# A decoder layer in one core: the sweep in pieces of 384 or 272 tokens, and the cross branch's output projection moved behind it

## The chip, the cores and the metric

The kernel runs on one core of a Trainium2 chip. The metric is the device time of one execution in microseconds; lower is better. The engines are TensorE (PE; its weight loads are listed as PEld), VectorE (DVE), ScalarE (ACT), GpSimd (POOL) and the queue engine SP. Each runs its own instructions in their order. DMAs are issued from SP, ACT and POOL, and a DMA that has to wait holds up what stands behind it on the engine that issues it.

## What is computed

One layer of a decoder with three parallel branches, for 2048 prompt tokens and 32 sample tokens (T = 2080 in all), in float32. Cut to what matters:

```
h = rmsnorm(x, g_pre) @ w_in          # 1024 -> 9472 columns: q k v za | ub zb | qc zc | gt
oa = three dilated window attentions per head, combined          # 12 heads x 64
ob = silu(layernorm(causal_conv(glu(ub))))                       # 768 channels
oc = softmax(qc @ mem_k.T) @ mem_v                               # 4 heads x 128, 256 memory rows
gates = sigmoid(gt)                                              # 3 x 1024
mix = (gates[0] * ((oa * silu(za)) @ w_pa)
     + gates[1] * ((ob * silu(zb)) @ w_pb)
     + gates[2] * ((oc * silu(zc)) @ w_pc))
y = x + rmsnorm(mix @ w_out, g_post)
```

The outputs are y, the new rows of keys and values, the convolution's state and the memory keys and values. Branch A is the attention, B the convolution, C the cross-attention; the numbers 0, 1 and 2 of the code stand for them. The sigmoids come out of tanh: a gate is held as tanh(x / 2), and one is added where it is used; factors of a half cancel in the last normalization.

## The kernel before, in words

Everything lies with channels on the 128 partitions and tokens along the free axis. Each float32 matrix product is done as three fast ones: both sides are split into a high and a low half, and `gemm` (lines 156 to 164) adds hi x hi, hi x lo and lo x hi in one PSUM tile, three matmuls for each 128 rows of the contraction. The weights of a block of 128 output columns are loaded and split by `load_w` (lines 141 to 154; the high half on POOL or ACT, the low one on POOL).

- **Phase A1** normalizes x into tiles x0 to x2 (three thirds of the tokens: 768, 768, 544) and runs the blocks of w_in for q, k, v, the convolution's input and qc, with pieces of 384, 256 or 288 tokens (`CHUNKS`, tile `g`). The second and third third of x are also kept in DRAM (`d_x`).
- **The sweep** (`sweep`, lines 1064 to 1081) runs the other 40 blocks of w_in: za (6), zb (6), zc (4), gt (24), over the thirds one after the other, each block again for each third. It takes `SCHUNKS`, seven pieces of 256 tokens and one of 288; each is 24 matmuls in tile `gg`. `chunk` evicts a piece: gt by one tanh on ACT (line 237), z blocks by a tanh on ACT (239) and a multiplication on VectorE (240), into tile `st` and from there to DRAM (242, on ACT's queue): `d_za`, `d_zb`, `d_zc`, and `d_g`, which has 8 tiles for each branch. `st` and the PSUM pool of `gg` have two buffers each. At a change of third the tiles x0h0 to x0h7 and x0l0 to x0l7 are loaded again by POOL's queue (1072).
- **Beside the sweep** run the convolution's normalization and the memory attention, the attention of the sample tokens, and then the prompt's attention, 12 heads in six pairs. At the end of a pair its three patterns are weighted: an exponential (422), coefficients to DRAM (430), from there into `cb` (437), multiplications, and a store to `d_act` (443).
- **Phase C** (`phase_c`) goes over four parts of 512, 512, 512 and 544 tokens. In each part it takes the branches in the order C, B, A: it loads the branch's output (`araw`, 1125) and its gate path (`z`, 1127), multiplies (1128), splits the product into `ac` tiles (1186, 1187), and for each of 8 blocks of columns loads a weight block (`craw`, 146; `chi`, `clo` 150, 151), multiplies in tile `pg`, and adds gate times product to `mix` (1139 for C, 1142 and 1144 for B and A). Behind the last branch come the product with w_out (tile `y`) and the normalization.

What sets the order: the instructions are written in program order (memory, sample attention, attention, sweep, phase C), and a scheduler that works from a simulated timeline sets them in the order of each engine. What was written earlier goes first when it is ready, and the sweep fills the rest. `d_` tensors lie in DRAM.

## Time and profile before

| | us |
|---|---|
| median of 3 runs | 3169.32 (3164.48 to 3171.83) |
| the profiled execution | 3156.1 |
| its span, first to last instruction | 3154.0 |
| TensorE busy | 2992.8 |
| VectorE / POOL / ACT busy | 2037.6 / 1368.9 / 1123.6 |
| sweep matmuls (tile gg), 7680, time with one running | 1092.6, between 850 and 2557 |
| phase C's first matmul | 2558.8 |

A row of a group gives the line, the engine, the operation, what it writes and reads, the shape and the count; behind the bar the time in which one ran, the mean of one in ns, and the engine's idle time just before such instructions with what ended it. Matmuls overlap in the pipeline, so the mean of one is longer than the distance to the next. Rows of stretches give start and end, length, then for each engine the busy time and the count, the clock that was granted to TensorE, the share of the 16 DMA engines and GB/s. Rows of the timeline give start, length, engine, line, operation, operands, count and in brackets the idle time before with what ended it; a q behind the engine (ACTq) is its sequencer that issues a DMA. Rows of waits give sum, times and longest.

### The profile page before, as it was taken

How to read it: one execution, taken by the hardware profiler on the slowest of the kernel's cores; microseconds unless marked ns; L12 is line 12 of the kernel's file. 1: busy time of each engine (PE TensorE's matmuls, PEld its weight loads, DVE VectorE, ACT ScalarE, POOL GpSimd, SP SyncE). 2: the span in 40 equal slices, each digit the busy share in tenths (PEclk: the TensorE clock that was granted, in tenths of full speed). 3: DMA queues.
4: the chain of work that ended last, by engine and by line, in shares of the span. 5: the costliest groups of instructions: out<-in, count | busy, mean ns of one | idle time of the engine just before them, and what ended most of it. 6: DMA issues, size and time to landing. Idle time of an engine off the chain costs nothing. (4 is left out here: it accounts for less than half of the span.)

```text
span 3154.0 us, 55551 instructions
## 1 busy us (share of the span) xinstructions
PE 2992.8 (95%) x20705; PEld 2837.2 (90%) x20705; DVE 2037.6 (65%) x3854; ACT 1123.6 (36%) x2835; POOL 1368.9 (43%) x1048
## 2 busy tenths in 40 slices
PE   7999999999977999999999999999999989999998
PEld 6899999999977899998999999999898967787897
DVE  5297797797677825565546667565757557555663
ACT  5110010010132423244447575665565532222221
POOL 0121322232455537444366666667776443233240
PEclk9999999999998999999999999999999999999999
DMA  6332222221255444468454556575655486657561
GB/s 224 111 100 83 80 60 61 63 63 64 90 162 166 127 140 144 147 213 251 144 142 118 151 139 159 123 196 144 166 140 149 117 283 210 226 172 220 158 206 53
DMA packets 532219, 454.67 MB, mean 144 GB/s; under 512 B 118191, under 2 KB 458581, under 8 KB 531137
## 3 DMA queue, kind: packets, MB, share of 16 engines
q1 hardware_dynamic: 357502, 335.36, 36.3%
q10 hardware_dynamic: 169840, 105.02, 11.6%
q0 software_dynamic: 4608, 10.75, 1.1%
q8 instruction: 164, 2.69, 0.4%
q14 instruction: 105, 0.86, 0.1%
HBM read 332.96 MB, written 118.04 MB: 143 GB/s over the span
## 5 line engine op out<-in xcount | busy, mean ns | idle before, releaser
L162 PE MATMUL gg<-x0h,whi 128*128 128x256 f32 (+1 forms) x2560 | 747.9, 292 | 33.9 <-DVE st L240 26.9
L164 PE MATMUL gg<-x0h,wlo 128*128 128x256 f32 (+1 forms) x2560 | 741.1, 290 | 5.7 <-POOL wlo L56 5.7
L163 PE MATMUL gg<-x0l,whi 128*128 128x256 f32 (+1 forms) x2560 | 742.3, 290 | 0.0
L55 POOL TENSOR_SCALAR whi<-wraw 128x1024 fp32r<-128x1024 f32 x162 | 221.4, 1368 | 918.0 <-PE g L163 534.7
L162 PEld LDWEIGHTS gg<-x0h,whi 128*128 128x128 f32 x2560 | 493.7, 193 | 42.2 <-DVE st L240 23.5
L164 PEld LDWEIGHTS gg<-x0h,wlo 128*128 128x128 f32 x2560 | 493.6, 193 | 8.3 <-POOL wlo L56 6.1
L163 PEld LDWEIGHTS gg<-x0l,whi 128*128 128x128 f32 x2560 | 493.9, 193 | 1.9 <-issue 0.3
L316 DVE SCALAR_TENSOR_TENSOR acc<-G,cw,acc 128x1536 f32<-128x1536 f32 (+15 forms) x354 | 461.8, 1336 | 0.0
L56 POOL TENSOR_TENSOR wlo<-wraw,whi 128x1024 fp32r<-128x1024 f32 x162 | 451.8, 2790 | 9.9 <-PE gg L164 0.5
L151 POOL TENSOR_TENSOR clo<-craw,chi 128x768 fp32r<-128x768 f32 (+1 forms) x96 | 172.6, 1799 | 352.9 <-ACT chi L150 338.1
L616 ACT ACTIVATE P<-T,stm 128x128 f32<-128x128 f32 (+1 forms) x576 | 260.7, 455 | 116.7 <-DVE stm L614 78.1
L233 ACT ACTIVATE st<-g 128x384 f32<-128x384 f32 (+1 forms) x132 | 60.3, 461 | 564.8 <-PE g L164 564.8
L614 DVE CUSTOM_DVE_ANT_0 T<-s,bias 128x128 f32<-128x128 f32 (+1 forms) x576 | 191.8, 357 | 78.3 <-PE s L606 44.6
L162 PE MATMUL pg<-ac,chi 128*128 128x512 f32 (+1 forms) x640 | 227.7, 358 | 14.9 <-ACT chi L150 7.9
L164 PE MATMUL pg<-ac,clo 128*128 128x512 f32 (+1 forms) x640 | 227.8, 358 | 6.2 <-POOL clo L151 6.2
L163 PE MATMUL pg<-ac,chi 128*128 128x512 f32 (+1 forms) x640 | 227.7, 356 | 0.7 <-DVE ac L1187 0.7
L164 PE MATMUL g<-x1h,wlo 128*128 128x384 f32 x544 | 186.2, 343 | 0.0
L163 PE MATMUL g<-x1l,whi 128*128 128x384 f32 x544 | 185.9, 342 | 0.0
L162 PE MATMUL g<-x1h,whi 128*128 128x384 f32 x544 | 183.0, 339 | 3.0 <-ACT x1h L131 3.0
L163 PE MATMUL g<-x0l,whi 128*128 128x384 f32 x544 | 184.9, 340 | 0.0
L164 PE MATMUL g<-x0h,wlo 128*128 128x384 f32 x544 | 183.7, 338 | 0.0
L162 PE MATMUL g<-x0h,whi 128*128 128x384 f32 x544 | 182.5, 337 | 0.0
(329 smaller groups left out, 7453.4 us busy)
## 6 DMA issues: line engine op xcount, KB each, us to landing
wraw<-in_w_in ACTq DMA_DIRECT2D x119, 512.0 KB
d_g<-st ACTq DMA_DIRECT2D x168, 128.0 KB
cb<-d_cf SPq DMA_DIRECT2D x72, 256.0 KB
g<-d_g SPq DMA_DIRECT2D x72, 256.0 KB
wraw<-in_w_in SPq DMA_DIRECT2D x35, 512.0 KB
kvc<-in_cache_k_win SPq DMA_DIRECT2D x8, 1536.0 KB
kvc<-in_cache_v_win SPq DMA_DIRECT2D x8, 1536.0 KB
raw<-d_q SPq DMA_DIRECT2D x48, 256.0 KB
```

The source lines that it names most:

```text
L55: nc.gpsimd.tensor_scalar(hi, raw, 1.0, 1.0, op0=ALU.mult, op1=ALU.mult)
L56: nc.gpsimd.tensor_sub(lo, raw, hi.bitcast(F32))
L151: nc.gpsimd.tensor_sub(lo, raw, hi.bitcast(F32))
L162: nc.tensor.matmul(ps, hi[:, k, :], h, start=k == 0, stop=False)
L163: nc.tensor.matmul(ps, hi[:, k, :], l, start=False, stop=False)
L164: nc.tensor.matmul(ps, lo[:, k, :], h, start=False, stop=k == kb - 1)
L233: nc.scalar.activation(st[:, :n], p[:, :n], AF.Copy, scale=sc)
L316: nc.vector.scalar_tensor_tensor(a3[:, lo:hi], G[:, src:src + hi - lo, 2 - m:130 - m], w, a3[:, lo:hi], op0=ALU.mult, op1=ALU.add)
L614: nc.vector.tensor_tensor_reduce(sc[:, :w], t[:, o:o + w], bias[:, 256 - w:256], 1.0, 3.0e38, ALU.add, ALU.min, m)
L616: nc.scalar.activation(P[:, o:o + w], sc[:, :w], AF.Exp, bias=m, scale=-1.0, accum_out=self.stl[:, col:col + 1])
```

## The change

`SCHUNKS` now has four pieces of 384 tokens and two of 272, two pieces in each third. Branch C's projection is taken out of phase C. A new function `branch_c` runs it behind the sweep, in the sweep's tiles: for each third it loads the four outputs of the cross-attention into x0h4 to x0h7 and the four gate paths into x0l4 to x0l7 (POOL's queue), multiplies, and splits into x0h0 to x0h3 and x0l0 to x0l3; for each of 8 column blocks it loads and splits a weight block in the sweep's weight tiles, and for each piece it loads the gate into an `st` tile (ACT's queue), does 12 matmuls in `gg`, multiplies in the `st` tile and stores it to the new DRAM tensor `d_mix` (ACT's queue). Phase C loads `mix` from `d_mix` beside branch B's gates and adds B and A to it.

```diff
-SCHUNKS = [(256 * i, 256) for i in range(7)] + [(1792, 288)]
+SCHUNKS = [(384 * i, 384) for i in range(4)] + [(1536, 272), (1808, 272)]
...
+    def branch_c(self, xp, wp, stg, ps):
+
+        nc, I = self.nc, self.I
+        for th, (a, n) in enumerate(THIRDS):
+            acts = []
+            for k in range(4):
+                raw, z, h, l = (xp.tile([128, 768], R32, name=t)[:, :n]
+                                for t in (f"x0h{4 + k}", f"x0l{4 + k}", f"x0h{k}", f"x0l{k}"))
+                raw, z = raw.bitcast(F32), z.bitcast(F32)
+                nc.gpsimd.dma_start(raw, self.d_act[12 + k][:, a:a + n])
+                nc.gpsimd.dma_start(z, self.d_zc[k][:, a:a + n])
+                nc.vector.tensor_mul(raw, raw, z)
+                nc.scalar.activation(h, raw, AF.Copy)
+                nc.vector.tensor_sub(l, raw, h.bitcast(F32))
+                acts.append((h, l))
+            for cb in range(8):
+                raw = stg.tile([128, 8, 128], F32, name="wraw", bufs=2)[:, :4]
+                hi, lo = (wp.tile([128, 8, 128], R32, name="w" + c)[:, :4] for c in ("hi", "lo"))
+                nc.scalar.dma_start(raw, I["w_proj_c"][0, :, 128 * cb:128 * cb + 128].rearrange("(k p) n -> p k n", p=128))
+                self.split_pool(hi, lo, raw)
+                for s, m in SCHUNKS:
+                    if a <= s < a + n:
+                        g = stg.tile([128, 384], F32, name="st")
+                        nc.scalar.dma_start(g[:, :m], self.d_g[16 + cb][:, s:s + m])
+                        p = ps.tile([128, 512], F32, name="gg")
+                        self.gemm(p[:, :m], (hi, lo), [(h[:, s - a:s - a + m], l[:, s - a:s - a + m]) for h, l in acts])
+                        nc.vector.scalar_tensor_tensor(g[:, :m], g[:, :m], 1.0, p[:, :m], op0=ALU.add, op1=ALU.mult)
+                        nc.scalar.dma_start(self.d_mix[cb][:, s:s + m], g[:, :m])
+                        yield
...
+                    if br == 1:
+                        nc.sync.dma_start(mix[cb][:, :n], self.d_mix[cb][:, s:s + n])
...
-                for bi, (br, k0, kb, wn) in enumerate(((2, 12, 4, "w_proj_c"), (1, 6, 6, "w_proj_b"), (0, 0, 6, "w_proj_a"))):
+                for br, k0, kb, wn in ((1, 6, 6, "w_proj_b"), (0, 0, 6, "w_proj_a")):
...
-                            if bi == 0:
-                                nc.vector.scalar_tensor_tensor(mix[cb][:, o:o + m], g[:, :m], 1.0, p[:, :m],
-                                                               op0=ALU.add, op1=ALU.mult)
-                            else:
-                                nc.vector.scalar_tensor_tensor(g[:, :m], g[:, :m], 1.0, p[:, :m],
-                                                               op0=ALU.add, op1=ALU.mult)
-                                nc.vector.tensor_add(mix[cb][:, o:o + m], mix[cb][:, o:o + m], g[:, :m])
+                            nc.vector.scalar_tensor_tensor(g[:, :m], g[:, :m], 1.0, p[:, :m], op0=ALU.add, op1=ALU.mult)
+                            nc.vector.tensor_add(mix[cb][:, o:o + m], mix[cb][:, o:o + m], g[:, :m])
...
                     self.fill(1000)
+                    for _ in self.branch_c(x0, wp, gp, pgg):
+                        pass
             self.phase_c()
```

The scheduler sets all engines anew, so three places of the order are shown. The first is TensorE where the fifth pair of heads ends and the sixth, the last, begins (line 388 turns the new pair's bias tiles; `o`, `pt` and `s` are attention). Before, pieces of the sweep lie around it:

```order
L164 MATMUL gg<-x0h_28426,wlo 128x288
L586 MATMUL o<-ph,V 128x256
L388 MATMUL pt<-ph,perm 128x512
L162 MATMUL gg<-x0h_28398,whi 128x256
L163 MATMUL gg<-x0l_28400,whi 128x256
L164 MATMUL gg<-x0h_28398,wlo 128x256
L162 MATMUL gg<-x0h_28402,whi 128x256
L587 MATMUL o<-pl,V 128x256
L586 MATMUL o<-ph,V 128x128
```

Now the last matmul of the sweep stands there (272 columns), six matmuls of the attention behind it, and then the new branch, whose tiles have been loaded anew:

```order
L164 MATMUL gg<-x0h_26162,wlo 128x272
L586 MATMUL o<-ph,V 128x256
L388 MATMUL pt<-ph,perm 128x512
L587 MATMUL o<-pl,V 128x256
L586 MATMUL o<-ph,V 128x128
L587 MATMUL o<-pl,V 128x128
L389 MATMUL pt<-pl,perm 128x512
L162 MATMUL gg<-x0h_28680,whi 128x384 x2
L163 MATMUL gg<-x0l_28681,whi 128x384
L164 MATMUL gg<-x0h_28680,wlo 128x384
```

Before, the sweep went on through the sixth pair and behind it. Now the branch runs beside the sixth pair, 12 matmuls of it between some 20 of the attention in the thirds of 384 tokens and some 12 in the last.

The second place is ACT late in the attention. Before, a piece of the sweep is a tanh (237) and a store (242) between the exponentials (616) and copies (564, 631):

```order
L237 ACTIVATE st<-gg 128x256
L616 ACTIVATE P,stl<-T,stm 128x128 x3
L242 DMA d_g_135<-st 128x256
L616 ACTIVATE P,stl<-T,stm 128x128 x2
L631 ACTIVATE ot<-o 64x512
L564 ACTIVATE ph<-pt 128x512
L616 ACTIVATE P,stl<-T,stm 128x128 x3
L564 ACTIVATE ph<-pt 128x512
L237 ACTIVATE st<-gg 128x288
```

Now there is no tanh, and a piece is a load of the gate (1106) and a store (1110); the load reuses a buffer whose store must have been read out:

```order
L1110 DMA d_mix_153<-st 128x384 x2
L616 ACTIVATE P,stl<-T,stm 128x128
L631 ACTIVATE ot<-o 64x512
L616 ACTIVATE P,stl<-T,stm 128x256
L1106 DMA st<-d_g_146 128x384
L564 ACTIVATE ph<-pt 128x512
L1101 DMA wraw<-in_w_proj_c 128x4x128
L631 ACTIVATE ot<-o 64x512
L616 ACTIVATE P,stl<-T,stm 128x256 x2
L1106 DMA st<-d_g_146 128x384
```

The third place is SP at the end of the attention, where the last pair's coefficients are stored (430) and read back (437). Before, between them stand weight blocks of branch C, and 346 matmuls of the sweep follow the attention's last one on TensorE:

```order
L1127 DMA z<-d_zc_91 128x512
L430 DMA d_cf_113<-ew 32x3x128
L146 DMA craw<-in_w_proj_c 128x4x128 x2
L437 DMA cb<-d_cf_113 64x1024 x4
L146 DMA craw<-in_w_proj_c 128x4x128
L437 DMA cb<-d_cf_113 64x1024 x6
L443 DMA d_act_119<-O 128x1024
L437 DMA cb<-d_cf_113 64x1024 x2
L443 DMA d_act_119<-O 128x1024
```

Now the loads of branch B's outputs stand between them, the sixth behind the second group of `cb`, and 72 matmuls of the new branch follow the attention's last one. The exponential (422) that the coefficients need stands on ACT behind the branch's last store:

```order
L430 DMA d_cf_113<-ew 32x3x128
L1157 DMA araw<-d_actb 128x512
L146 DMA craw<-in_w_proj_b 128x6x128
L1157 DMA araw<-d_actb 128x512
L437 DMA cb<-d_cf_113 64x1024 x4
L1159 DMA z<-d_zb_86 128x512
L1157 DMA araw<-d_actb 128x512
L1159 DMA z<-d_zb_87 128x512
L146 DMA craw<-in_w_proj_b 128x6x128 x2
L437 DMA cb<-d_cf_113 64x1024 x2
L1157 DMA araw<-d_actb 128x512
```

3 lines of the change are left out of this document (2 added, 1 removed).

## The prediction

> **What bounds the kernel now.** I read the page's first lines, then the groups of instructions with their forms kept apart, then the timeline of TensorE, then the same views cut into stretches, and last the waits.
>
> ```profile
> span 3154.0 us, 55551 instructions
> PE 2992.8 (95%) x20705; PEld 2837.2 (90%) x20705; DVE 2037.6 (65%) x3854; ACT 1123.6 (36%) x2835; POOL 1368.9 (43%) x1048
> ...
> L162 PE MATMUL gg<-x0h,whi 128*128 128x256 f32 x2240 | 651.2, 291 | 31.7 <-DVE st L240 25.6 <-DMA x0h<-d_x 4.7 <-POOL whi L55 1.1
> L162 PE MATMUL gg<-x0h,whi 128*128 128x288 f32 x320 | 96.7, 302 | 2.3 <-DVE st L240 1.2 <-ACT st L237 1.1
> ```
>
> TensorE is busy 95% of the span, the next engine 65%: the sum of TensorE's work sets the time. The sweep (tile gg) has 2560 matmuls on each of lines 162 to 164, 7680 in all. But 291 ns is not what one of them costs, because they overlap. The price of one is the distance from start to start, in the timeline of TensorE:
>
> ```profile
> 301.28 0.33 PE L163 MATMUL g<-x0l,whi 128*128 128x384 f32 x1
> 301.46 0.33 PE L164 MATMUL g<-x0h,wlo 128*128 128x384 f32 x1
> ...
> 1152.31 0.28 PE L162 MATMUL gg<-x0h,whi 128*128 128x256 f32 x1
> 1152.43 0.28 PE L163 MATMUL gg<-x0l,whi 128*128 128x256 f32 x1
> ...
> 2512.06 0.29 PE L163 MATMUL gg<-x0l,whi 128*128 128x288 f32 x1
> 2512.19 0.30 PE L164 MATMUL gg<-x0h,wlo 128*128 128x288 f32 x1
> ...
> 2760.46 0.39 PE L163 MATMUL pg<-ac,chi 128*128 128x512 f32 x1
> 2760.69 0.39 PE L164 MATMUL pg<-ac,clo 128*128 128x512 f32 x1
> ...
> 3005.17 0.29 PE L164 MATMUL pg<-ac,clo 128*128 128x272 f32 x1
> 3005.29 0.28 PE L162 MATMUL pg<-ac,chi 128*128 128x272 f32 x1
> ```
>
> So a matmul of 256 columns takes 0.120 us, 272 0.125, 288 0.133, 384 0.174 and 512 0.231 (each pair's distance, read over its neighbours to the ns). From 256 to 512 columns the cost grows by 0.111 us; 256 columns at that rate are 0.111 and leave about 0.01 us that each matmul pays whatever its width. Fewer, wider matmuls save that.
>
> Four stretches of the same execution, busy time by engine, then the granted clock, the DMA share and the rate:
>
> ```profile
> 850.00:1150.00 300.00, 250.39 (x1879) 241.40 (x1878) 215.06 (x277) 101.52 (x189) 151.87 (x140) 0.93 0.49 150
> 1560.00:2500.00 940.00, 903.83 (x7418) 891.78 (x7418) 591.22 (x1762) 569.67 (x1738) 604.67 (x485) 0.99 0.57 143
> 2504.00:2559.00 55.00, 48.26 (x366) 47.51 (x365) 21.85 (x20) 9.62 (x22) 30.91 (x17) 0.97 0.78 224
> 2714.70:2806.70 92.00, 88.66 (x383) 71.36 (x382) 55.73 (x71) 28.16 (x42) 43.66 (x23) 1.00 0.69 213
> ```
>
> In the first, TensorE idles 50 us. In the second (prompt attention with the sweep between) it is 96% busy. The third is the rest of the sweep after the attention's last matmul. The fourth is the projections of one part of phase C, at full width.
>
> **The sweep's wider pieces.** A weight block had seven pieces of 256 and one of 288, at 24 matmuls each; it gets four of 384 and two of 272. Over 40 blocks: 40 x 24 x [(7 x 0.120 + 0.133) - (4 x 0.174 + 2 x 0.125)] = 960 x 0.027 = **25.9 us less**. It lies on the engine that sets the time, so I take it whole. The Trainium skill prices this otherwise: its page TensorE: Matmul & The Clock Gate, section Back-to-back issue gap, gives N / 2.4 + 2.5 ns for a matmul behind another, and by that estimate the same bracket is worth 5 ns and the whole edit 4.8 us. The rows above stand against it here.
>
> Fewer pieces also hand over fewer PSUM buffers. The pool has two, and in the blocks za, zb and zc a buffer is free only when VectorE has run line 240:
>
> ```profile
> PE gg L162 <- DVE st L240: 23.4, 12, 4.6
> PE sco L664 <- DVE sm L662: 14.1, 6, 5.6
> ```
>
> (waits of TensorE in the stretch 850 to 1150: sum, times, longest). The piece that runs meanwhile covers 24 x 0.174 = 4.2 us instead of 2.9, so each of the 12 waits, 1.95 us on average, should shrink by 1.3, and a quarter of the handovers goes: about 6 us of 23.4 would stay. VectorE is busy 72% of that stretch and still has the rest to do, so I count **12 us less** (bounds 0 and 18).
>
> **The cross projection leaves phase C.** Per part it is a quarter of 384 matmuls. At 92.0 us for the part shown that is 23.0; I take 23.0 twice, 192 x 0.125 = 24.0 for the part of 272, and 96 x 0.231 = 22.2 for the first part, whose ramp is counted below: **92.2 us less**. Its acts, gates, weight splits and additions were beside other work there. The eight loads of mix per part replace those of g, acts and weights for this branch: 2 MB for 6 MB.
>
> **It comes back in the sweep's pieces.** Three thirds of eight blocks, 12 matmuls a piece: 8 x 12 x (4 x 0.174 + 2 x 0.125) = **90.8 us more**. The two moves nearly cancel; what counts is what the new place waits for.
>
> *Its start.* The loads go into tiles x0h4 to x0l7, which the last piece of the sweep still reads, by POOL's queue. The nearest rows are the sweep's own change of third (POOL's issue, TensorE's first use, and the median to landing of those loads):
>
> ```profile
> 1452.14 0.75 POOL L1072 DMA_DIRECT2D x0l<-d_x  x1 [0.40 <-PE gg L164]
> ...
> 1462.57 0.38 PE L162 MATMUL gg<-x0h,whi 128*128 128x256 f32 x1 [2.53 <-DMA x0h<-d_x]
> ...
> x0l<-d_x POOLq DMA_DIRECT2D x8, 384.0 KB, 10.3
> ...
> x0l<-d_x POOLq DMA_DIRECT2D x8, 272.0 KB, 5.8
> ```
>
> That is 10.4 us from issue to use; here a multiplication, a rounding on ACT and a subtraction follow, some 3 us by these rows of phase C at two thirds of the width:
>
> ```profile
> L1128 DVE SCALAR_TENSOR_TENSOR araw<-araw,z 128x512 f32<-128x512 f32 x48 | 43.4, 911 | 41.6 <-DMA araw<-d_act 21.1 <-DMA araw<-d_actb 16.8 <-issue 2.3
> L1187 DVE TENSOR_TENSOR ac<-araw,ac 128x512 fp32r<-128x512 f32 x48 | 43.1, 905 | 10.9 <-ACT ac L1186 7.2 <-PE y L1168 3.0
> ```
>
> In the sweep attention matmuls fill such a hole. At this start the order has only six between the sweep's last matmul and the new branch's first, because a pair of heads ends there. So TensorE stands some 11 us, and then gets a slice of the acts every 2.4 us where it needs 1.0: **14 us more** (9 if the loads land as the 272 KB ones did, 20 if each row is late). The Trainium skill, page DMA: Bandwidth & Descriptors, section Anatomy of one DMA, puts a load on this queue at 2.0 us plus bytes / 436e3, 2.9 us for 384 KB; by it the term would be about 7. The rows say 10.3. At the two later thirds the loads lie under the matmuls before, only rounding and subtraction stand out: **3 us more** (0 to 6).
>
> *Its pace.* Each piece loads a gate slice into st, multiplies there and stores it; st has two buffers. So a buffer's round is a load, 12 matmuls, VectorE, a store. A store's landing shows where the sweep's end ran into phase C's loads (ACT's timeline):
>
> ```profile
> 2521.17 0.36 ACTq L242 DMA_DIRECT2D d_g<-st  x1
> ...
> 2526.88 0.41 ACT L237 ACTIVATE st<-gg 128x288 f32<-128x288 f32 x1 [2.47 <-DMA d_g<-st]
> ```
>
> 5.3 us from the issue's end to the slot's next use, at 224 GB/s. In the whole trace such waits make 25.2 us, 15.7 of them in the stretch 2500 to 2560 (ACT's waits, first the whole, then that stretch):
>
> ```profile
> ACT st L237 <- DMA d_g<-st: 25.2, 9, 4.4
> ...
> ACT st L237 <- DMA d_g<-st: 15.7, 6, 4.4
> ```
>
> So at the attention's 143 GB/s a store lands sooner; no row gives the load. I put each at half of 5.3, an estimate: with VectorE and two issues the round is some 6.5 us. The order leaves a buffer about 8.6 us in the thirds of 384 (two pieces of 2.1 us and some 40 attention matmuls) and 5.8 in the last, whose 16 pieces would come 0.35 us late each, 6 us. What waits then is ACT, with the attention's exponentials behind the issue, and VectorE at line 1109 with scores and splits behind it. I take **8 us more**; bounds 0, and 38 if each of 48 pieces is 0.8 us late. The issues themselves: ACT gets 120 more for the branch and 80 fewer stores of the sweep, 40 at 0.36 us, 14 us on an engine that is 61% busy there; POOL gets 24 of 0.75 at most, 18 us, with the splits of V and of weights behind them, at 64%. Neither is the end of a path by these shares, so they cost nothing of their own; without that slack they are inside the bound of 38.
>
> *The end of the attention and phase C's ramp.* Before, 359 matmuls of the sweep run after the attention's last one, 45 us at their prices in 55, so 9 are lost, and the first part of phase C takes 110.4 us where 384 x 0.231 = 88.7 would do:
>
> ```profile
> 2559.00:2669.40 110.40, 99.25 (x384) 76.08 (x384) 15.40 (x23) 0.92 0.81 259
> ```
>
> (tile pg alone), 22 more lost. In the changed order only 72 matmuls are behind the attention, six pieces and 9 us; with loads and stores at 5 us they take about 25, 16 lost. Then branch B needs six acts, not four, and SP issues the last of them behind the loads of cb that end the last pair of heads. Before, that chain ran under the sweep:
>
> ```profile
> 2517.62 0.52 ACT L422 ACTIVATE ew<-ew 32x384 f32<-32x384 f32 x1 [0.65 <-DVE ew L421]
> ...
> 2527.59 3.34 SPq L437 DMA_DIRECT2D cb<-d_cf  x4
> ...
> 2559.85 0.34 SPq L443 DMA_DIRECT2D d_act<-O  x1
> ```
>
> 42 us from the exponential to the last store. Now the exponential stands on ACT behind the branch's last store. With the loads of cb some 10 us after it and one more round for B's sixth act, TensorE has the first three blocks complete 22 us after the tail for 12.5 us of work; a late weight block and branch A's last act cost perhaps 11 more. That is 16 + 10 + 11 = 37, and 2 of the steady losses, against 31: **8 us more** (bounds -10 and 20).
>
> Sum: -25.9 - 12 - 92.2 + 90.8 + 14 + 3 + 8 + 8 = -6.3. The profiled execution took 3156.1 us, 2.1 around its span of 3154.0; the median of the runs shown is 3169.3, so the same difference gives **3163 us**.
>
> **The rivals.** (1) *More is won.* The PSUM waits shrink by 18, the start costs 9 and the pace and the later thirds nothing: -25.9 - 18 - 1.4 + 9 + 8 = -28, **3141**. For it: the 96% of the attention's stretch, so the order is good at filling. Against it: the order at the start. (2) *The gate's round trip decides*, slower: two buffers of st with a DMA on each side, from the point where load plus store land later than about 7.5 us together. At 0.8 us a piece the term of 8 becomes 38: +24, **3193**. For it: 5.3 us for one store under load. Against it: that load is not the attention's. (3) *The last pair's chain is bare*: SP's loads for B and A wait until cb and d_act are through, the 8 of the ramp becomes 25: +11, **3180**. (4) *The change doesn't do what it says*: width alone sets the sweep's time, the sweep saves nothing: +20, **3189**. The rows at 0.120 and 0.174 speak against it. The figure of the Trainium skill's page TensorE: Matmul & The Clock Gate, cited above, lies nearer to this case than to the rows.
>
> **How the numbers follow.** Forecast 42%, rival 1 20%, 2 22%, 3 11%, 4 5%. A measurement of this kernel can tell about 0.2%, 6.3 us, from no change, and the forecast lies on that edge: of its 42 I count 23 faster, 17 the same, 2 slower; of rival 3 four the same, of rival 4 one. Faster 43%, same 22%, slower 35%. The range goes from below rival 1 to rival 2, 3134 to 3195; the forecast's own is 3148 to 3170.
>
> **What would show it.** Sweep matmuls start 0.174 us apart at 384 columns, and the waits on line 240 fall below 12 us. A gap of 10 us or more before the first matmul on the new branch's x0h0. Waits of ACT and VectorE on the loads of st: under 15 us in sum for the forecast, over 40 for rival 2. A part of phase C between 68 and 72 us of projections, the first near 95. The forecast is wrong if the sweep's and the branch's matmuls together, by their distances, are not about 24 us less than before, or if TensorE's share in the attention falls under 94%.

## The result and the profile after

The changed kernel takes 3180.4 us (median of 19 executions, 3173.1 to 3187.5), the kernel before on the same chip 3166.9 (19 executions, 3152.0 to 3180.3). The ratio is 1.0052, 95% interval 1.0039 to 1.0065: **slower by 0.5%, some 16 us**, where 0.2% less was forecast. The profiled execution of before took 3156.1 us and so lies 11 us below its median, the one of the changed kernel lies on it with 3180.3, so differences of time are taken from the ratios, in us by 3167, and the profiles say only where the time lies.

The first lines of the page after:

```profile
span 3178.6 us, 51540 instructions
PE 2983.0 (94%) x18881; PEld 2828.8 (89%) x18881; DVE 2004.8 (63%) x3822; ACT 1094.8 (34%) x2719; POOL 1402.5 (44%) x1088
```

TensorE is busy for 10 us less than before and the span is 25 us longer. By stretches (as before: start and end, length, busy time and count of each engine, granted clock, DMA share, GB/s) the early sweep is better, the attention's 974 us are worse, and one short stretch inside them and three behind them are much worse:

```profile
850.00:1150.00 300.00, 265.83 (x1606) 256.60 (x1606) 203.34 (x261) 102.67 (x180) 163.32 (x146) 0.95 0.51 158
1666.00:2640.00 974.00, 911.77 (x6711) 893.05 (x6712) 608.62 (x1780) 560.41 (x1697) 621.65 (x527) 0.96 0.60 157
...
2460.00:2500.00 40.00, 27.05 (x99) 21.95 (x100) 26.14 (x56) 9.33 (x30) 16.41 (x22) 0.62 0.84 253
...
2640.00:2665.00 25.00, 11.77 (x76) 10.60 (x74) 6.28 (x15) 1.92 (x4) 3.17 (x3) 0.78 0.63 186
2665.00:2700.00 35.00, 18.29 (x56) 12.29 (x56) 22.53 (x24) 7.34 (x11) 10.04 (x5) 0.77 0.85 215
2700.00:2740.00 40.00, 21.95 (x83) 16.77 (x84) 28.95 (x28) 9.19 (x12) 14.95 (x8) 0.79 0.93 307
```

**2460 to 2500: the branch's start.** The sweep's last matmul stands at 2452.9. On TensorE's timeline six attention matmuls follow, then nothing for 5.6 us until the first activations are there, and then matmuls of 384 columns 0.32 us apart where the sweep has 0.174:

```profile
2452.86 0.29 PE L164 MATMUL gg<-x0h,wlo 128*128 128x272 f32 x1
...
2454.70 0.49 PE L389 MATMUL pt<-pl,perm 128*128 128x512 f32 x1 [0.90 <-POOL pl L56]
2460.81 1.01 PE L162 MATMUL gg<-x0h,whi 128*128 128x384 f32 x2 [5.62 <-ACT x0h L1095]
...
2462.29 0.52 PE L164 MATMUL gg<-x0h,wlo 128*128 128x384 f32 x1
2462.61 0.52 PE L163 MATMUL gg<-x0l,whi 128*128 128x384 f32 x1
```

VectorE's timeline shows why the next slices come late. The statistics of the fifth pair of heads (`mn`, line 418) stand in its order between the product of the third slice (1094) and its split (1096), and they wait 4.9 us for a load:

```profile
2465.50 0.94 DVE L1094 TENSOR_TENSOR x0h<-x0h,x0l 128x768 f32<-128x768 f32 x1
2471.34 0.28 DVE L418 TENSOR_TENSOR mn<-stc 32x128 f32<-32x128 f32 x1 [4.89 <-DMA stc<-d_st]
2471.55 0.94 DVE L1096 TENSOR_TENSOR x0l<-x0h,x0h 128x768 fp32r<-128x768 f32 x1
```

Then ScalarE. Its stores of the first pieces wait for VectorE, its gate loads wait for those stores, and it computes nothing for 16.2 us, until the next exponentials (616) of the attention:

```profile
2477.45 0.81 ACTq L1110 DMA_DIRECT2D d_mix<-st  x2
2481.27 1.49 ACTq L1106 DMA_DIRECT2D st<-d_g  x2
2485.34 4.77 ACTq L1110 DMA_DIRECT2D d_mix<-st  x2
2490.78 0.33 ACTq L1106 DMA_DIRECT2D st<-d_g  x1
2491.16 0.40 ACT L616 ACTIVATE P<-T,stm 128x128 f32<-128x128 f32 x1 [16.16 <-DVE stm L614]
```

That row names VectorE's scores (614) as what ended the wait, not the queue. The scores' matmuls had been done since 2446.7. What they lacked was the last bias tile of the pair: TensorE turned it (389) only behind the branch's first four pieces, and its copy (393) and the scores stand on VectorE behind two additions of the branch (1109) that waited for loads:

```profile
2482.81 0.40 PE L389 MATMUL pt<-pl,perm 128*128 128x512 f32 x1
2484.75 0.55 DVE L1109 SCALAR_TENSOR_TENSOR st<-st,gg 128x384 f32<-128x384 f32 x1 [3.87 <-DMA st<-d_g]
2489.20 0.56 DVE L1109 SCALAR_TENSOR_TENSOR st<-st,gg 128x384 f32<-128x384 f32 x1 [3.02 <-DMA cb<-d_cf]
2489.67 0.75 DVE L393 COPY bias<-pt 128x256 f32<-128x256 f32 x2
2490.33 0.28 DVE L614 CUSTOM_DVE_ANT_0 T<-s,bias 128x128 f32<-128x128 f32 x1
```

(The wait of 3.0 us is put down to a load of the old pair's coefficients, which the addition does not read, so what ended that one stays open.) So the branch held the pair of heads on TensorE and on VectorE. From 2483.2 to 2491.7 TensorE started four matmuls, and in the 40 us of the stretch 99.

**2640 to 2740: the end of the attention.** The attention's last matmul is at 2640, not 2506. The last pieces of the branch wait for their gates, and part of the last pair's combination (421) stands behind them on VectorE:

```profile
2654.06 0.44 DVE L1109 SCALAR_TENSOR_TENSOR st<-st,gg 128x272 f32<-128x272 f32 x1 [4.02 <-DMA st<-d_g]
2657.26 0.44 DVE L1109 SCALAR_TENSOR_TENSOR st<-st,gg 128x272 f32<-128x272 f32 x1 [2.76 <-DMA st<-d_g]
...
2662.74 0.44 DVE L1109 SCALAR_TENSOR_TENSOR st<-st,gg 128x272 f32<-128x272 f32 x1 [4.55 <-DMA st<-d_g]
2663.10 0.54 DVE L421 TENSOR_TENSOR ew<-stc,mn 32x384 f32<-32x384 f32 x1
```

SP's timeline then carries the chain on: the second `d_act` store is issued at 2711.0, and the loads of `mix` stand behind it:

```profile
2710.99 0.32 SPq L443 DMA_DIRECT2D d_act<-O  x1
...
2716.07 6.44 SPq L1150 DMA_DIRECT2D mix<-d_mix  x8
```

TensorE's waits from 2640 to 2790 have one of 17.5 us there, until VectorE's product with the gates (1170). The gate tiles `g` come free only after the addition to `mix`, at 2723.1; between that and the product, at 2734.3, VectorE also waits 3.8 us for `d_za`, so not all of the 17.5 us is due to `mix`. Before, the last `d_act` store (2559.9) came with the first projection of phase C (2558.8). Now it comes 45 us after it.

```profile
PE pg L162 <- DVE g L1170: 17.5, 1, 17.5
PEld pg L162 <- ACT ac L1213: 17.4, 5, 8.2
```

The parts of phase C, by tile pg alone, the first and the second:

```profile
2665.50:2775.00 109.50, 75.24 (x288) 56.92 (x288) 9.90 (x15) 0.85 0.91 280
2797.40:2886.00 88.60, 66.28 (x288) 53.68 (x287) 10.30 (x16) 1.00 0.67 213
```

A full part has fallen from 88.7 us of busy time to 66.3. The first one, with a quarter less to do, takes as long as before.

### The profile page after: what moved, and what is told of

Read it like the earlier page. It is cut to its first block, busy times and chain, and to the rows that moved or that the text cites. A ratio compares the mean times of both kernels' runs of the same rounds, so it can differ in the third digit from the quotient of the medians.

```text
span 3178.6 us, 51540 instructions
## 1 busy us (share of the span) xinstructions
PE 2983.0 (94%) x18881; PEld 2828.8 (89%) x18881; DVE 2004.8 (63%) x3822; ACT 1094.8 (34%) x2719; POOL 1402.5 (44%) x1088
## 4 chain that ended last, share of the span: by engine, by line
PE 69%; DMA 13%; DVE 6%; POOL 5%; issue 4%; ACT 2%; SPq 1%; ACTq 0%; DVEq 0%; POOLq 0%
PE g L162 8%; PE g L163 8%; PE g L164 8%; PE gg L162 6%; PE gg L163 6%; PE gg L164 6%; PE pg L162 3%; PE pg L163 3%; PE pg L164 3%; DMA cb<-d_cf 2%; PE pt L560 2%; PE y L1196 2%; PE y L1195 2%; PE y L1194 2%; DMA wraw<-in_w_in 2%
## 5 line engine op out<-in xcount | busy, mean ns | idle before, releaser
L162 PE MATMUL gg<-x0h,whi 128*128 128x384 f32 (+1 forms) x2112 | 696.3, 330 | 51.8 <-DVE st L240 19.3
L163 PE MATMUL gg<-x0l,whi 128*128 128x384 f32 (+1 forms) x2112 | 690.9, 327 | 6.5 <-DVE x0l L1096 6.4
L164 PE MATMUL gg<-x0h,wlo 128*128 128x384 f32 (+1 forms) x2112 | 690.2, 327 | 0.0
L55 POOL TENSOR_SCALAR whi<-wraw 128x1024 fp32r<-128x1024 f32 (+1 forms) x186 | 254.7, 1370 | 957.0 <-PE g L163 527.0
L56 POOL TENSOR_TENSOR wlo<-wraw,whi 128x1024 fp32r<-128x1024 f32 (+1 forms) x186 | 484.9, 2608 | 14.0 <-PE gg L164 3.3
L162 PEld LDWEIGHTS gg<-x0h,whi 128*128 128x128 f32 x2112 | 404.7, 192 | 62.8 <-issue 14.5
L163 PEld LDWEIGHTS gg<-x0l,whi 128*128 128x128 f32 x2112 | 404.8, 192 | 11.2 <-DVE x0l L1096 9.7
L151 POOL TENSOR_TENSOR clo<-craw,chi 128x768 fp32r<-128x768 f32 x64 | 131.7, 2059 | 309.2 <-ACT chi L150 309.2
L162 PE MATMUL pg<-ac,chi 128*128 128x512 f32 (+1 forms) x480 | 170.7, 358 | 35.9 <-DVE g L1170 17.5
L163 PE MATMUL pg<-ac,chi 128*128 128x512 f32 (+1 forms) x480 | 170.2, 355 | 5.0 <-DVE ac L1214 4.9
L605 PE MATMUL s<-KH,QS 128*128 128x128 f32 (+1 forms) x576 | 161.4, 302 | 11.7 <-POOL QS L480 6.7
```

The costliest lines, as they stand in the source:

```text
L55: nc.gpsimd.tensor_scalar(hi, raw, 1.0, 1.0, op0=ALU.mult, op1=ALU.mult)
L56: nc.gpsimd.tensor_sub(lo, raw, hi.bitcast(F32))
L151: nc.gpsimd.tensor_sub(lo, raw, hi.bitcast(F32))
L162: nc.tensor.matmul(ps, hi[:, k, :], h, start=k == 0, stop=False)
L163: nc.tensor.matmul(ps, hi[:, k, :], l, start=False, stop=False)
L164: nc.tensor.matmul(ps, lo[:, k, :], h, start=False, stop=k == kb - 1)
```

## The experiments

Ratios are to the kernel before, run on the same chip in turn. All times are medians.

| run | what it is | ratio (95% interval) | us |
|---|---|---|---|
| the change | | 1.0052 (1.0039 to 1.0065) | 3180.4 |
| e1 | before, all pieces wide | 1.0086 (1.0061 to 1.0111) | 3191.1 |
| e2 | change, first 512 tokens of C in phase C | 1.0075 (1.0049 to 1.0101) | 3191.9 |
| e3 | change, eight gate buffers | 0.9998 (0.9977 to 1.0020) | 3162.8 |
| e4 | cross projection in both places | 1.0375 (1.0345 to 1.0404) | 3281.9 |
| e5 | change, last pair's weights early | 1.0030 (1.0012 to 1.0049) | 3176.7 |
| e6 | change without the branch's loads | 0.9936 (0.9913 to 0.9959) | 3149.1 |
| e7 | branch behind thirds 1 and 2 of the sweep | 1.0025 (1.0009 to 1.0042) | 3179.5 |
| e8 | e7, middle third in 256 | 0.9977 (0.9960 to 0.9994) | 3164.6 |
| e9 | change, branch 288 matmuls later | 1.0091 (1.0070 to 1.0112) | 3194.0 |
| e10 | e9 with eight gate buffers | 1.0034 (1.0020 to 1.0048) | 3178.1 |
| e11 | e6 with eight gate buffers | 0.9904 (0.9878 to 0.9930) | 3138.4 |
| e12 | e11 with the weights early | 0.9884 (0.9863 to 0.9906) | 3131.3 |
| e13 | before, first third's pieces wide | 0.9921 (0.9898 to 0.9945) | 3144.3 |
| e14 | e7, half of the middle third in 256 | 0.9926 (0.9904 to 0.9947) | 3147.8 |

### The wider pieces alone (e1)

On the kernel before:

```diff
-SCHUNKS = [(256 * i, 256) for i in range(7)] + [(1792, 288)]
+SCHUNKS = [(384 * i, 384) for i in range(4)] + [(1536, 272), (1808, 272)]
```

> The kernel before with the wider pieces alone: the cross branch stays in phase C. Theory 'sum of terms' (the terms of the prediction add up, each wherever it stands): -25.9 for the pieces and -12 for the early waits, 3129 us (3122 to 3145). Rival 'hole': the sweep's work ends a pair of heads earlier, since the order has no sweep matmul left beside the sixth pair, and the pair runs bare. The pairs take 152 us beside the sweep in the profile of before; bare it is bounded below by VectorE's share, about 115 us, of which TensorE has some 45 us of its own work; so 70 or more us are lost of what was won: 3190 us (3170 to 3230), and TensorE's busy share in the last 100 us of attention is under 0.7 with a granted clock under 0.95.

It took 3191.1 us, as the rival "hole" had it: 0.9% slower than the kernel before and no better than the changed one. The order leaves no sweep matmul beside the last part of the attention: the last one runs at 2453, the attention ends at 2565 (before: 2506). Its stretches:

```profile
2350.00:2450.00 100.00, 96.87 (x793) 96.86 (x794) 57.19 (x181) 65.57 (x198) 71.49 (x60) 0.98 0.52 125
2450.00:2550.00 100.00, 81.70 (x480) 72.89 (x479) 79.41 (x251) 70.40 (x226) 45.97 (x44) 0.78 0.40 87
```

The clock fell as expected, the busy share only to 0.82, since at a clock of 0.78 the same matmuls last longer; the count of matmuls, 480 against 793, says it better. Then phase C began with the last pair's combination still on VectorE, ahead of the first evictions (`mix`, 1139) in its order:

```profile
2604.91 2.28 DVE L442 TENSOR_TENSOR O<-O 128x1024 f32<-128x1024 f32 x1
...
2616.49 1.21 DVE L442 TENSOR_TENSOR O<-O 128x1024 f32<-128x1024 f32 x1
...
2620.32 1.88 DVE L1139 SCALAR_TENSOR_TENSOR mix<-g,pg 128x512 f32<-128x512 f32 x3
```

```profile
PE pg L162 <- DVE mix L1139: 28.1, 1, 28.1
```

The second fence is TensorE's wait in the same place. So the sweep is more than work: it is what TensorE does while the attention's chains run. A shorter sweep leaves a hole, and the branch was put into that hole. That is the setting for everything below.

### More cover from phase C (e2), and the branch in both places (e4)

e2 keeps the first 512 tokens of C in phase C and takes them out of `branch_c`:

```diff
-        for th, (a, n) in enumerate(THIRDS):
+        for th, (a, n) in enumerate(((512, 256), *THIRDS[1:])):
...
-                for s, m in SCHUNKS:
+                for s, m in [(512, 256)] if th == 0 else SCHUNKS:
...
-                    if br == 1:
+                    if br == 1 and s:
...
-                for br, k0, kb, wn in ((1, 6, 6, "w_proj_b"), (0, 0, 6, "w_proj_a")):
+                for br, k0, kb, wn in (((2, 12, 4, "w_proj_c"),) if not s else ()) + ((1, 6, 6, "w_proj_b"), (0, 0, 6, "w_proj_a")):
```

> The changed kernel, but the first 512 tokens keep their cross projection in phase C, as its first pass of 96 matmuls; the branch in the sweep's tiles does the other 1568 tokens. Theory 'tail' (the excess is lost where the last pair's sums are still being combined while phase C has only the second branch's 144 matmuls a pass to run): the waits between the branch's last matmul and the end of the first 288 projections, 43 us of them in the profile after, fall to some 15 to 22 as in the kernel before, 3155 us (3145 to 3165). Theory 'round trip' (the branch is paced by its two st buffers): a quarter fewer trips, about 5 us, 3175 us. Theory 'start' (the loads at the branch's first matmuls): the first third has 256 columns instead of 768, its loads land sooner, 5 to 10 us, 3171 us, and the gain is seen at 2450 to 2500 us and not behind 2650.

3191.9 us: it lost 7 more (the intervals overlap) instead of winning 25, and theory "tail" in this form fell. The 96 matmuls are there, but they cover nothing, for the reason seen in e1: four PSUM tiles fill, and then TensorE waits for VectorE, which has the last pair's combination first.

```profile
PE pg L162 <- DVE mix L1171: 26.0, 1, 26.0
```

e4 is the kernel before with the wide pieces and `branch_c` (the call and `d_mix` as in the change), its phase C untouched:

```diff
                     self.fill(1000)
+                    for _ in self.branch_c(x0, wp, gp, pgg):
+                        pass
```

> The cross projection is computed twice: in the sweep's tiles as in the changed kernel (its sums are stored and not read), and in phase C as in the kernel before. Against the changed kernel it shows what leaving phase C was worth, against the kernel before what the branch costs in its new place. The prediction's sum: 3167 - 38 + 115.8 = 3245, and the changed kernel is 65 to 84 below it. Theory 'tail': with the first 96 matmuls of phase C as cover again the ramp loses no more than before, so the changed kernel's gain from leaving is only 92 - 30 = 62: 3242 (3235 to 3250). Where the excess lies ahead of phase C ('start' or 'round trip'), leaving is worth the full 92 and more: 3272 (3262 to 3285).

3281.9 us, 102 above the changed kernel (1.0375 less 1.0052): leaving phase C was worth the full 92 and more, not 62. That agrees with an excess ahead of phase C; but phase C itself, with the work that it had before, took 611 us in e4's profile against 595, so not all of it lies there.

### The round trip of the gates (e3)

```diff
-                        g = stg.tile([128, 384], F32, name="st")
+                        g = xp.tile([128, 768], R32, name=f"x0{'hl'[gi % 2]}{4 + gi // 2 % 4}").bitcast(F32)
+                        gi += 1
```

> The changed kernel with the branch's gates and sums in eight buffers in place of two (the tiles that held its raw activations, which are idle by then). Theory 'round trip': the waits of VectorE and TensorE on st and d_g at 2500 to 2665 us (18.7 us of VectorE from 2640 on) go, and since the combining of the last pair stands behind them on VectorE and ScalarE's queue, its chain starts 20 us sooner: 3155 us (3145 to 3165). Theory 'tail' alone: the first loads and stores were hidden anyway, the ramp keeps its length: 3172 to 3180. Theory 'start': no change within 4 us of 3180.

0.9998, so 17 us are won back, as "round trip" had it. In the changed kernel VectorE waits 29.3 us for gate loads from 2500 to 2665; with eight buffers that group is gone. The waits of the changed kernel in that stretch:

```profile
DVE st L1109 <- DMA st<-d_g: 29.3, 16, 4.5
```

The attention ends at 2613 instead of 2640 and the last `d_act` store comes 20 us after the first projection, not 45. Phase C, from its first projection to the end, takes 496 us instead of 513. These two add up to more than 17 us: e3's profile took 3147.6 us, its median is 3162.8.

### The start (e6), and both together (e11)

e6 leaves the branch's activations out and multiplies the tiles that the sweep left:

```diff
-            acts = []
-            for k in range(4):
...
-                acts.append((h, l))
+            acts = [(self.X[2][0][k], self.X[2][1][k]) for k in range(4)]
...
+                        o = s - a if th == 2 else 0
-                        self.gemm(p[:, :m], (hi, lo), [(h[:, s - a:s - a + m], l[:, s - a:s - a + m]) for h, l in acts])
+                        self.gemm(p[:, :m], (hi, lo), [(h[:, o:o + m], l[:, o:o + m]) for h, l in acts])
```

> The changed kernel, but the branch multiplies what the sweep left in its tiles instead of loading, multiplying and splitting its own activations (its sums are not those of the cross branch; matmuls, gates and stores are all there). This takes away the start and both third boundaries together. The prediction priced them at 14 + 3: 3163 us. From the trace of the changed kernel (19.9 us of waits on x0h and x0l at 2400 to 2500, half clock behind them, 2.1 + 2.1 at the next boundary) 'start' is worth more: 3155 us (3148 to 3162). If the waits only move to the gates' round trip, which is as slow without the loads: 3172 to 3180.

0.9936: 37 us by the ratios, 31 by the medians, where the prediction had priced start and boundaries at 17. The stretch that had 99 matmuls at a clock of 0.62 has 229 (e6's stretches):

```profile
2460.00:2500.00 40.00, 36.19 (x229) 34.86 (x228) 30.10 (x96) 22.24 (x75) 19.42 (x18) 0.91 0.82 220
```

The attention ends at 2607, 33 us sooner; phase C has 512 us as in the changed kernel. With the waits e6 also takes away 22 us of VectorE's busy time (1982.9 for 2004.8) and the 24 loads' traffic; which of these counts most is not separated. e11 adds the eight buffers of e3 to e6.

> The run without loads and products (the branch multiplies what the sweep left, its sums are not those of the cross branch) with the eight buffers as well. Separate losses: 3149 - 17 = 3132 us (3126 to 3138). One loss seen twice (VectorE waits for loads of either kind): 3147 to 3150.

0.9904, 10 us below e6 (expected 17; the two intervals overlap, so 17 is not excluded). Start and round trip together cost 47 us. By the ratios some 7 us are counted in both e3 and e6, which would fit that both hold the same VectorE and the same queue of ScalarE, but 7 us is within the noise here.

### The last pair's combination (e5, e12)

On the changed kernel (e5) and on e11 (e12):

```diff
-                    src = self.d_cf[hp][g:g + 1, a * S + half * 1024:a * S + half * 1024 + 1024]
+                    src = self.d_cf[min(hp, 4)][g:g + 1, a * S + half * 1024:a * S + half * 1024 + 1024]
```

> The changed kernel, but the last pair of heads is combined with the weights of the pair before it, which are long stored: the loads of cb wait for nothing of the last pair (the last pair's outputs are weighted wrongly, everything is still computed and stored). In the profile after, the last pair's combination runs from 2640 to 2711 us, its weights are stored at 2670.6, and TensorE has 72 matmuls of the sweep's tiles left beside it. Theory 'combination' (the end of the last pair's combination, which in the kernel before ran beside 346 sweep matmuls, is bare now): the store of its output comes about 25 us sooner and so do the last projections of phase C's first pass: 3155 us (3145 to 3165). Rival (only the round trip of the gates counts, and the first 288 projections wait for something else): 3180, within 5 us.

> The run before it with the last pair of heads combined by the weights of the pair before (the sums are again not the reference's): nothing of the change's three losses is left, so it bounds what they cost together. Theory 'combination': phase C is 17 us shorter, as it was in the run with the early weights alone, and since no gates are waited for now, nothing of it is given back ahead of phase C: 3115 us (3110 to 3122). If the gain is given back again: 3126 to 3132.

By the ratios both won 6 to 7 us (1.0030 against 1.0052, 0.9884 against 0.9904), with intervals that overlap those of the runs they change: not 25 and not 17, and zero is not excluded. By its median e12 came out where it was expected "if the gain is given back again". The store moved as meant, to 4 us before the first projection in e5 and 2 in e12, and phase C shortened by 18 us (495) and 20 (491). But the attention itself ended later, at 2651 instead of 2640, and at 2620 instead of 2606. The scheduler set other rows anew as well, and what delays the attention there is not settled: the net price of the bare combination is some 7 us in these orders.

### Moving the branch later (e9, e10)

e9, on the changed kernel (e10 is the same on e3):

```diff
-            for kind, j in blocks:
+            for bi, (kind, j) in enumerate(blocks):
...
-                for s, m in SCHUNKS:
+                for s, m in (SCHUNKS if th != 1 or bi < 28 else [(768 + 256 * i, 256) for i in range(3)]):
```

> The changed kernel, but the last 12 of the 40 weight blocks of the sweep's middle third go in pieces of 256 again: 288 more sweep matmuls, 4 us of TensorE time, and so the branch begins 288 sweep matmuls later in the order, inside the last pair of heads: of the first 60 matmuls from its start 51 are the pair's, where the changed kernel has 9; and 312 of the sweep's and branch's matmuls are left behind attention in place of 72. The buffers are the changed kernel's. Theory 'place' (the start is dear because it falls where one pair of heads ends and TensorE has nothing else; the last pair's combination is bare because little is left behind it): 4 paid, some 20 of the start's 33 us and some 13 of the combination's 18 won back, 3151 us (3140 to 3162). Rival 'price' (the 24 loads, products and splits cost VectorE and the queues the same wherever they stand): 3184 us.

> The run before it with the gates and sums in eight buffers as well. If the round trip of the gates and the place of the start are two separate losses: 17 below the run before it, 3134 us (3125 to 3145), which would beat both kernels by 1 per cent. If with more matmuls around them the two buffers were no longer waited for: the same as the run before it within 4 us.

The start was better (209 matmuls in the 40 us from 2480, at a clock of 0.91), phase C's ramp too: 480 us from the first projection instead of 513. And still the run was 12 us slower than the change by the ratios, worse than even the rival "price" had it. The 312 matmuls left behind the attention are the branch's own, and there nothing runs beside them. e9 from the attention's end to phase C, and TensorE's wait there:

```profile
2592.00:2710.00 118.00, 64.19 (x316) 59.81 (x315) 37.79 (x55) 10.85 (x15) 35.01 (x29) 0.78 0.72 216
```

```profile
PE gg L162 <- DVE st L1111: 40.2, 15, 6.5
```

118 us for matmuls that need 39 to 54 (312 at 0.125 to 0.174). Eight buffers (e10) won 18 us here, as much as in e3, but not the 3134 us hoped for. The wait was another then: the next third's activations, no longer hidden, as e10's waits behind the attention show. Part of it the eight buffers make themselves: they are the tiles into which the next third's activations are loaded, and POOL's issues of those loads (1093 and 1094 in e10) waited 3.8 and 7.6 us in all for the landing of stores out of them.

```profile
PE gg L162 <- ACT x0h L1096: 21.6, 5, 10.3
```

"Place" fell: moving the branch away from the pair's boundary only moved its waits to where they are bare. As a filler the branch is worse than the sweep, which loads nothing for a piece and evicts its gt blocks on ScalarE.

### Sweep blocks behind the attention instead of the branch (e7, e8, e14)

`sweep` calls the branch for the third that it has just finished, thirds 1 and 2 only; the last part of phase C (the last third's tokens) computes C itself; gates in eight buffers as in e3:

```diff
                         self.chunk(kind, j, s, m, w, stg, ps, "gg", q=nc.scalar)
                         yield
+            if th < 2:
+                yield from self.branch_c(xp, wp, stg, ps, (th,))
```

e8 sweeps the middle third in pieces of 256, e14 the last 20 of its 40 blocks.

> The cross projection of the first two thirds (1536 tokens) runs right behind the sweep's own blocks of that third, with eight buffers for the gates; the last 512-token part of phase C computes it itself; so what is left for the last pair of heads is sweep blocks, which ScalarE evicts, 73 matmuls of them behind attention. Sum: -23 for the pieces, -10 for the early waits, +69 for the branch, -82 for three parts of phase C, +20 for the two starts = -26. Theory 'combination': 73 matmuls are 9 us of cover where the kernel before had 42, so 30 come back: 3170 us (3158 to 3178). Theory 'round trip only': the sum stands, 3140 (3132 to 3150).

> As the run before it, with the middle third swept in pieces of 256 as in the kernel before: 13 us more TensorE time, and 702 sweep matmuls behind attention in place of 73. Theory 'combination': the 30 us of the run before it are covered again and 13 are paid: 17 us below it, 3153 us (3143 to 3163). Theory 'round trip only': 13 us above it.

> The cross projection of the first two thirds right behind the sweep's blocks, as in the run with 73 matmuls behind attention (1.0025 of before) and the one with 702 (0.9977), but with half of the middle third's blocks in pieces of 256: 374 sweep matmuls behind attention, as many as the kernel before has. Theory 'filler': the cover is whole with 350 and each narrow block beyond costs 0.33 us for nothing, so it is 6.6 us below the run with 702: 3157 us (3150 to 3165), ratio 0.996. If cover beyond that still pays: not below 3165.

The three differ in how many sweep matmuls are left behind the attention: 73, 702 and 374. They took 1.0025, 0.9977 and 0.9926. e7 is at the slow end of "combination"; e8 lies 15 us below it although it has 13 us more to do, as "combination" had it; e14 lies 16 below e8, where narrower blocks beyond the cover were priced at 6.6. So a kernel with the branch can lie below the one before, by 23 us, once sweep blocks stand behind the attention. That the branch itself pays is not shown by this: e14 also has wider pieces, and no run has e14's pieces with the cross projection in phase C. In e14 TensorE is whole at the end of the attention (2577):

```profile
2500.00:2600.00 100.00, 99.70 (x821) 99.46 (x821) 47.88 (x147) 53.73 (x160) 49.01 (x36) 1.00 0.43 127
```

### Wide pieces in the first third only (e13)

On the kernel before:

```diff
-SCHUNKS = [(256 * i, 256) for i in range(7)] + [(1792, 288)]
+SCHUNKS = [(0, 384), (384, 384), (768, 256), (1024, 256), (1280, 256), (1536, 256), (1792, 288)]
```

> The kernel before with pieces of 384 in the sweep's first third alone; the cross projection stays in phase C. 109 sweep matmuls are left behind attention where the kernel before has 346 and the run with all pieces wide had none and a bare pair of heads. The wider pieces of a third are worth 13 of the 26 us, and the waits on ScalarE's and VectorE's st stand in that third: 8 to 10 us. Theory 'filler' (the wider sweep is worth its sum as long as it still reaches to the end of attention; what falls short of the last pair's combination comes back as idle TensorE): -13 - 8 + 10 (13 us of cover in place of 42, the combination's 18 us bare for a good half) = -11, 3156 us (3148 to 3164). If the pieces had been worth nothing by themselves: 3167 and more.

0.9921, 25 us won where 11 were expected: one line is worth as much as the best version with the branch whose output is that of the layer (e14; their intervals overlap). In the profiles the sweep ends at 2533 instead of 2557, and phase C with its shorter cover takes 607 us instead of 595; the spans differ by 9 us, near the expected 11. Where the rest of the 25 us of the ratio lies, these two profiles cannot show. The waits on line 240 fell as the prediction had it (23.4 us in twelve before, in the stretch 800 to 1200 of e13):

```profile
PE gg L162 <- DVE st L240: 12.4, 3, 9.1
```

## Why the prediction was wrong

The step that failed is the branch's waits in its new place: the terms *Its start* (14, bounds 9 and 20, and 3 for the later thirds) and *Its pace* (8). They were priced at 25 us together, and taking both out won 47 (e11 against the change). The rest of the sum, taken as a whole, came out as priced, though not each of its terms:

| terms of the prediction | priced, us | measured, us | by |
|---|---|---|---|
| start and later thirds | +17 | +37 (31 by medians) | e6 against the change |
| pace of the st round trip | +8 | +17 alone, +10 beside the other | e3, e11 |
| both | +25 | +47 | e11 against the change |
| end of the attention and ramp | +8 | +6 to +7, for the late weights alone | e5, e12 |
| pieces, early waits, matmuls out of C and back | -39.3 | -37 | e12 against before |
| sum | -6.3 | +16 | the change |

The measured sum closes by construction, as its rows are the distances of one run to the next. The prediction's 8 is a difference to the losses of the kernel before, while e5 and e12 only take one wait away, so that row compares unlike things.

The account also depends on the order in which the edit is taken apart. Taken first, the pieces and the early waits (e1) were priced at -38 and measured +27, and the branch on top of them won 11 where the sum had 32 lost. Both ways say the same: the sweep was what TensorE did beside the attention's chains, the sum took its shortening whole, and the branch that came in its place filled the hole, but with waits of its own.

*Pieces and early waits.* Their prices were right. The distances are 0.174 at 384 columns as said, and 0.126 at 272. The waits on line 240 from 850 to 1150 came to 13.1 us in two waits (under 12 was the mark, narrowly missed). But the two terms could not be had by themselves: e1 shows that they take away cover, which the sum did not say. The formula that the prediction cited from the Trainium skill, page TensorE: Matmul & The Clock Gate, section Back-to-back issue gap, gives 162.5 ns at 384 columns and 115.8 at 272, and the section calls it the gap of an isolated matmul, not of a stream with weight loads; the trace has 174 and 126, and the rows decide.

*The matmuls' move.* A full part of phase C came to 65 to 66 us from first to last projection, better than the 68 to 72 forecast; the first took 109.5 where 95 was the mark. The two errors cancel: from the first projection to the end 595 us became 513, 82 less, and 92.2 less 8 had been forecast. So the ramp was mis-sized too, by 14 us, and the other three parts together by about as much the other way (27 us each where 23 to 24 had been said).

*The start.* Its first half was seen rightly in kind: TensorE stood 5.6 us ahead of the branch's first matmul, 8 us behind the sweep's last (a gap of 10 to 11 had been said), and the slices came late one after the other. What was missing is that the bounds stopped at the fourth slice. VectorE and ScalarE work in order, and on both the branch's rows stand among those of the pair of heads that was to cover it. VectorE stood 4.9 us at the old pair's statistics with a slice ready behind, and 3.9 and 3.0 us at the branch's additions with the new pair's scores behind; the bias tile that those scores needed was turned behind the branch's first pieces; ScalarE had no exponential to run for 16.2 us; and TensorE, short of work, ran at a clock of 0.62. The cover and what it was to cover stopped together. That these terms were summed one by one, each with the attention running on beside it, is the mistake.

*The pace.* The round was estimated at 6.5 us against the 5.8 that the order leaves in the last third, and the waits of VectorE on gate loads came to 33.2 us in the whole trace, between the 15 and the 40 that were to tell forecast from rival. What a late gate costs was taken as its own lateness. It also holds ScalarE's queue and, at the end, the last pair's combination behind it on VectorE. That is the likely way in which 8 became 17; the runs show the 17, not how it divides.

*The rivals.* Rival 3 named 3180 us and the bare chain, and the chain was bare: the store 45 us behind the first projection. But by e5 and e12 that costs some 7 us and not 25; the time agreed by luck and the cause did not. Rival 2 named the smaller part of the cause, at half its price (17 us against 38); no rival named the start as dear. The condition that was to show the forecast wrong did: TensorE's share in the attention, 911.8 of 974 us, is 93.6%, under 94 (before: 96). A small slip: the 359 sweep matmuls that the prediction put behind the attention's last one are counted from 2504; from that one on, at 2506, there are 346.

## What to carry to other kernels

Work that fills gaps is priced by what it waits for, not by its length: a filler with loads, multiplications and a store for each piece takes its place in the same in-order queues as the chain it is to cover, and here both stopped together. Before shortening or replacing a filler, look at what it still covers at its end; here the cheap gain was a shorter sweep only as far as it still reached to the end of the attention (e13), and the kernels with the branch came out below the one before only with many sweep blocks left behind the attention (e8, e14). And a stall should be priced to the point where the engines behind it are level again, not to the first instruction that runs.

## What the runs showed of the hardware

- The clock granted to TensorE fell with its idle time and made it dearer: after 5.6 us without a matmul the 384-column matmuls started 0.32 us apart instead of 0.174, and the stretch of 40 us had a clock of 0.62; without the branch's loads (e6) it was 0.91. The Trainium skill, page TensorE: Matmul & The Clock Gate, Part 1: The HAM clock gate, says that the array drops to 1.2 GHz after about 3.4 us of idling; 384 / 1.2 GHz is 0.32 us, and the trace agrees. For the return to full speed the Trainium skill names about 3.4 us of sustained work in the same part; here the distance came back to 0.17 us at 2479.9, 7 us after the last gap of more than 1 us (it ended at 2472.5), and the measurement decides.
- A DMA issue that waits holds the compute of its engine. From 2500 to 2665 of the changed kernel ScalarE's copies of the attention's outputs (631), which use nothing of the branch, waited four times, 8.9 us in all, until a store of the branch had landed: issues of the branch stood ahead of them in ScalarE's order, among them a gate load for the buffer that the store had to leave.

```profile
ACT ot L631 <- DMA d_mix<-st: 8.9, 4, 4.4
```
